# Hybrid-attention trunk: how scores' keys and queries lie in HBM, buffer counts and planner delays

## The chip, the cores and the metric

One NeuronCore of a Trainium2 chip runs the whole program. TensorE (PE) multiplies, with its weight loads shown apart (PEld); VectorE (DVE), ScalarE (ACT) and GpSimd (POOL) do elementwise work; SyncE (SP) issues most DMAs, and GpSimd issues some too. The metric is the device time in microseconds, the median of several runs.

## The reference

One decoder layer on 1024 tokens of width 1024, all in fp32: a norm, one input projection of 2956 columns, three kinds of causal attention with heads of 64, an output projection, a norm and an MLP with a squared ReLU.

```python
h = rms_norm(x, norm_mix);  a_q, a_kv, a_g, b_qkv, c_qkv = split(h @ w_in)
o_a = nsa_mixer(...)             # 4 heads: compressed, selected and windowed keys
o_b = dilated_mixer(...)         # 6 heads in 3 groups, strides 1, 4, 16
o_c = stick_breaking_mixer(...)  # 6 heads: sigmoid weights, running products
x = x + concat(o_a, o_b, o_c) @ w_out
x = x + square(relu(rms_norm(x, norm_mlp) @ w_up)) @ w_down
```

A score of the dilated and stick-breaking heads is q·k over 64 dimensions, for 128 queries by up to 512 keys.

## The kernel before

**Precision.** Each fp32 operand of a matmul is split into a high and a low part of type float32r (`put`, L106): ScalarE makes the high part by a cast (L103), VectorE or GpSimd the low one by a subtraction (L112; L114 with a factor). A product is then three matmuls. For scores (`scores`, L632) the 64 dimensions leave half of the 128 partitions free, so the keys' tile holds the high parts in partitions 0 to 63 and the low parts in 64 to 127. One query tile holds the high part twice, the other the low part twice, and two matmuls (L639, L642) give all four products.

**Stages.** Half 0 means tokens 0 to 511, half 1 the rest. First come input, norm statistics and the first projections (to 50 us). Then the projections of both halves run beside the attention of half 0 (to about 470 us); then the output projection and the MLP of half 0 beside the attention of half 1 (to about 1000 us); then the rest of that MLP, and output projection and MLP of half 1 alone. The projections are matmuls of L250 and L258, the MLP's of L1094 and L1160.

**Through HBM.** Projected q and k of the dilated and stick-breaking heads go to `q_d` and `k_d` in HBM (`spill_qk`, L538: one store of 128 x 512 for the high part, one for the low, rows being two heads of 64), v to `v_d`. The queries of the first mixer's half 1 go to `nq_d`. They come back later as loads issued by GpSimd (`load_heads`, L597; `Nsa.load`): keys by a pattern whose first dimension is high or low (2) and the second the 64 rows, queries by one whose first dimension repeats the same 64 rows (2, step 0), values as 128 plain rows. The loads go to tiles of a pool with 11 slots of 4 KB a partition.

**Raw weights.** `load_w` (L141) fetches a weight group in 2 or 4 parts of 256 KB through 2 raw buffers (`wraw`); a part is asked for by SP, split, and the buffer taken for the part two further on.

**Order.** The Python program plans with a model clock in units of about a microsecond of TensorE. Attention is a list of units: `Sb` (stick-breaking, 256 queries of a head), `Dil` (a dilated head, half of the tokens), `Nsa` (128 queries of two heads). All other matmul work is one generator, the filler, and `spend` gives the filler so many units for each unit of attention, by what is left of both (0.4 to 4). A unit may be loaded when what it needs is in the set `done` (`later` puts it there after a delay) and enough slots are free; its scores come `WAIT` = 8.5 units after the load (`prefetch`, `ready`), and `fill` puts filler there. The framework's scheduler then orders each engine's queue, and every engine and DMA queue works in order.

Of the kernel before, what the change touches and what calls it, by code (L numbers as in the profile page):

```python
# [10 lines left out]
F32 = mybir.dt.float32  # L11
# [4 lines left out]

S, D, HD, DFF = 1024, 1024, 64, 4096
NB = S // 128
EPS = 1e-6
WMAX = 268  # L20
# [39 lines left out]
def tile_trunk(ctx, tc, x, xT, w_in, w_out, w_up, w_down, cw1, cw2, small, t_nsa, t_dil, out):  # L60
# [57 lines left out]
    hctx = ExitStack()  # L118
    slots = actx.enter_context(tc.tile_pool(name="slots", bufs=11))
    ckp = actx.enter_context(tc.tile_pool(name="ck", bufs=10))  # L120
# [20 lines left out]
    def load_w(key):  # L141
# [23 lines left out]
        def load(part):  # L165
            dst = part[1]
            m = dst.shape[1] * (dst.shape[2] if len(dst.shape) == 3 else 1)
            raw = wpool.tile([128, 2 * WMAX], F32, tag="wraw", bufs=2, name="wraw")[:, :m]
            i = nc.sync.dma_start(raw, src[:, part[0]:part[0] + m])
            if clock[0] < 10.0:  # L170
                in_order(i)
            return raw.rearrange("p (k c) -> p k c", c=128) if len(dst.shape) == 3 else raw

        raws = [load(p) for p in parts[:2]]

        def split():
            for i, (_, hi, lo) in enumerate(parts):
                put(hi, lo, raws[i], pool=i % 2 == 1 and len(w_keys) < 14)
                if i + 2 < len(parts):
                    raws.append(load(parts[i + 2]))  # L180
                if i % 2:
                    yield
# [27 lines left out]
    pending = []  # L210
    DMA, SB0 = 4.0, 8.0
    FLIP, START, END = 1.3, 5.0, 2.5
    SLOTS = 11
    live = [2]
# [214 lines left out]
    def nsa_q(W_q, half):  # L429
        v2 = []  # L430
        for i in range(2):
            v2.append((yield from normed_blocks(W_q, 256, 4, 4 * half + 2 * i)))
        if half == 0:
            yield from take(4)

        def fin(p):
            tp = pair_T(v2, 128 * p)
            if half == 1:
                hi, lo = [sg_t("tnq", F32R)[:, :512] for _ in range(2)]
                for i, r in ((0, A), (1, B)):  # L440
                    put(hi[r], lo[r], tp[r], qg[r, 2 * p + i:2 * p + i + 1])
                for part, t in enumerate((hi, lo)):
                    nc.sync.dma_start(nq_d[p, part].rearrange("h d t -> (h d) t"), t.bitcast(F32))
                return
            nsa['q', 0, p] = hi, lo = [slot(n).rearrange("p (h t) -> p h t", h=2) for n in ("nqh", "nql")]
            for i, r in ((0, A), (1, B)):
                put(hi[A, i], lo[A, i], tp[r], qg[r, 2 * p + i:2 * p + i + 1])
                nc.scalar.copy(hi[B, i], hi[A, i].bitcast(F32))
                nc.vector.tensor_copy(lo[B, i], lo[A, i].bitcast(F32))
        for p in range(2):  # L450
            later(6.0, lambda p=p: fin(p))
# [84 lines left out]


    def spill_qk(pair, j, cs, hi, lo):  # L538
        for part, t in enumerate((hi, lo)):
            nc.sync.dma_start((q_d, k_d)[j][pair, part, :, cs], t.bitcast(F32))  # L540

# [50 lines left out]

    def rows_of(t, *dims):

        return bass.AP(tensor=t.tensor, offset=t.offset, ap=[list(d) for d in dims])

    def load_heads(pair, half, heads=(0, 1)):  # L597

        q0, nk = 512 * half, 512 * (half + 1)
        ks = slice(0, nk)  # L600
        n = len(heads)
        hs = slice(heads[0], heads[0] + n)
        halves = lambda t: t.rearrange("p (h s) -> p h s", h=2)
        part, twice = (128 * S, 2), (0, 2)
        if n == 1:
            r = 64 * heads[0]
            qq = halves(slot("qq"))
            for i in range(2):
                nc.gpsimd.dma_start(qq[:, i], rows_of(q_r[pair, i, r:r + 64, q0:q0 + 512], twice, (S, 64), (1, 512)))
# [5 lines left out]
            nc.gpsimd.dma_start(k, rows_of(k_r[pair, 0, r:r + 64, ks], part, (S, 64), (1, nk)))  # L615
            nc.gpsimd.dma_start(v, v_r[pair, heads[0], :, ks])
            return [(qq[:, 0], qq[:, 1], k, v)]
        qh, ql = [halves(slot(nm)) for nm in ("qh", "ql")]
        k, v = [[t[:, 0], t[:, 1]] if half == 0 else [t, slot(nm)]
                for nm in "kv" for t in [halves(slot(nm)) if half == 0 else slot(nm)]]  # L620
        for i, t in enumerate((qh, ql)):
            for h in heads:
                r = 64 * h
                nc.gpsimd.dma_start(t[:, h], rows_of(q_r[pair, i, r:r + 64, q0:q0 + 512], twice, (S, 64), (1, 512)))
        for h in heads:
            r = 64 * h
            nc.gpsimd.dma_start(k[h], rows_of(k_r[pair, 0, r:r + 64, ks], part, (S, 64), (1, nk)))
        for h in heads:
            nc.gpsimd.dma_start(v[h], v_r[pair, h, :, ks])
        return [(qh[:, h], ql[:, h], k[h], v[h]) for h in heads]  # L630

    def scores(qh, ql, n, k, masked=False):  # L632

# [4 lines left out]
        cs = slice(128 * n, 128 * n + 128)  # L638
        nc.tensor.matmul(o, qh[:, cs], k, start=True, stop=False)  # L639
        if masked:  # L640
            nc.tensor.matmul(o[:, w - 128:w], ident_r, ahead, start=False, stop=False)
        nc.tensor.matmul(o, ql[:, cs], k, start=False, stop=True)  # L642
        return ps
# [101 lines left out]
    class Nsa(Unit):  # L745
# [8 lines left out]
        def load(self):  # L754
            if self.slots:
                qs = nsa['q', 1, self.hp] = [slot(nm).rearrange("p (h t) -> p h t", h=2) for nm in ("nqh", "nql")]
                for part, t in enumerate(qs):
                    for i in range(2):
                        nc.gpsimd.dma_start(t[:, i], rows_of(nq_r[self.hp, part, i], (0, 2), (512, 64), (1, 512)))

# [6 lines left out]
        def branch(self, i, chunks, kt, vt, gate, l0):  # L767

            n, h = self.n, 2 * self.hp + i
            (qh, ql), sl, st = [t[:, i] for t in nsa['q', self.half, self.hp]], SLOPES[6 + h], self.st[i]  # L770
            prev = None
            for k, (p, c0, tab) in enumerate(chunks):
                w = p.shape[-1]
                acc = st[:, 4 * l0 + k:4 * l0 + k + 1]
                ps = scores(qh, ql, n % 4, kt[:, c0:c0 + w])
                biased(ps, w, tab, sl, p, acc, prev)
# [55 lines left out]
    class Sb(Unit):  # L832
# [16 lines left out]
        def weights(self, n, c0):  # L849

            qh, ql, k, _ = self.head
# [4 lines left out]
            ps = scores(qh, ql, n % 4, k[:, c0:c0 + w], masked=after is None)  # L856
            nc.scalar.activation(b[:, :w], ps[:, :w], AF.Sigmoid, scale=-0.125)
# [37 lines left out]
    class Dil(Unit):  # L895
# [18 lines left out]
        def probs(self):  # L914
# [9 lines left out]
            for ro in range(4):  # L924
# [9 lines left out]
                for g in (1, 2):  # L934
                    qh, ql, k, _ = hd[g]
                    if half == 0:
# [4 lines left out]
                    acc = acc_t[:, ro:ro + 1] if g == 1 else stP[:, ro, 0:1]  # L941
                    biased(scores(qh, ql, ro, k), w, dtab[:, 256 * g - w:256 * g], 4.0 * sl[g], p, acc, prev)
                    prev = acc
# [8 lines left out]
            nc.sync.dma_start(self.oN, dP.rearrange(nat, p=128))  # L952
            qh, ql, k, _ = hd[0]
            for i in range(4):
# [5 lines left out]
                p = pn[-1][:, 256 * (i % 2):256 * (i % 2) + w]  # L960
                ps = scores(qh, ql, i, k[:, c0:c0 + w])
                biased(ps, w, dtab[:, 256 - w:256], sl[0], p, stN[:, i, 0:1], None)
# [74 lines left out]
    def raw_tile():  # L1037
        if 'mp' in late:
            return late['mp'].tile([128, 512], F32, tag="raw", bufs=4, name="raw")
        return wpool.tile([128, 2 * WMAX], F32, tag="wraw", bufs=2, name="wraw")[:, :512]  # L1040

# [160 lines left out]
    def flag(key):  # L1202
        later(0.0, lambda: done.add(key))

# [7 lines left out]
    def filler():  # L1212
# [7 lines left out]
        in_order(nc.sync.dma_start(dtab, t_dil))  # L1220
        later(SB0, lambda: done.add(('sb', 0)))
        W = next_w()
# [14 lines left out]
        for key, half in per_half:  # L1237
# [52 lines left out]

    LEAD, WAIT, LEAST, MOST = 0.8, 8.5, 0.4, 4.0
    debt = [0.0]
# [168 lines left out]
```

## Time and profile before

| | |
|---|---|
| median of 3 runs | 1473.87 us (1472.23 to 1474.32) |
| profiled execution | 1478.49 us, span 1476.7 us, mean granted clock 0.953 |
| TensorE busy | 1347.3 us (91%) |
| weight loads / VectorE / ScalarE / GpSimd busy | 1156.5 / 836.8 / 647.7 / 684.3 us |
| SP's DMA queue / GpSimd's DMA queue | 136.45 MB / 33.85 MB |

TensorE is the busiest engine, but its share is an average over the stages. "Idle" of an engine in a stretch is the stretch's length less its busy time. [...] "Landing" of a DMA is the time from its issue to the moment when its last byte is told.

### The profile page before, as it was taken

The page shows a single profiled execution, that of the slowest core. Times are in us where ns is not written, and L with a number is a line of the kernel's source. Part 1 is how long each engine was busy: PE and PEld are TensorE (multiplying, and loading weights), DVE is VectorE, ACT ScalarE, POOL GpSimd, SP SyncE. Part 2 cuts the span into 40 slices and gives each one's busy share as a digit, 9 for nine tenths or more (in the row PEclk, how much of TensorE's full clock was granted, in tenths as well). Part 3 has the DMA queues.
Part 4 walks back from the last instruction along what each step waited for, and adds up shares of the span by engine and source line. Part 5 has one row for each costly group of instructions (what it writes and reads, how often), then busy time and mean ns, then how long its engine had stood idle before and what let it go on. Part 6 is the DMA issues. An engine that isn't in the chain of part 4 may idle for free.

```text
span 1476.7 us, 21132 instructions
## 1 busy us (share of the span) xinstructions
PE 1347.3 (91%) x7241; PEld 1156.5 (78%) x7241; DVE 836.8 (57%) x1973; ACT 647.7 (44%) x1453; POOL 684.3 (46%) x614
## 2 busy tenths in 40 slices
PE   8887978688797999999997696999999999999998
PEld 6876978688786887888886585788888888888887
DVE  7365664468566998888885353783453332332333
ACT  6234554357454666555564142553343222222221
POOL 2123224434673424454556252534755555556553
PEclk9999989899798999999999798999999999999999
DMA  5697566852734422244548545224434333333332
GB/s 180 166 187 192 143 148 152 152 134 61 136 95 144 137 62 61 73 119 115 122 113 146 94 110 110 75 62 136 123 111 145 89 100 94 92 100 92 95 100 86
DMA packets 178572, 171.65 MB, mean 116 GB/s; under 512 B 89376, under 2 KB 105248, under 8 KB 178464
## 3 DMA queue, kind: packets, MB, share of 16 engines
q1 hardware_dynamic: 91808, 136.45, 32.5%
q0 software_dynamic: 86656, 33.85, 13.0%
q8 instruction: 57, 0.93, 0.3%
q14 instruction: 51, 0.42, 0.1%
HBM read 142.67 MB, written 27.30 MB: 115 GB/s over the span
## 4 chain that ended last, share of the span: by engine, by line
PE 67%; DMA 13%; DVE 11%; issue 4%; ACT 4%; SPq 1%; POOL 1%; DVEq 0%; ACTq 0%; POOLq 0%
PE pd L1094 25%; PE pd L1160 23%; DMA wraw<-in_w_in_dram 6%; PE pd L250 6%; PE ptp L684 3%; DMA k<-k_d 2%; PE pd L258 2%; PE po L705 2%; PE po L700 2%; PE pscore L642 1%; PE pscore L639 1%; DMA xch<-stx 1%; DMA wraw<-in_cmp_w_dram 1%; ACT whi L103 1%; DVE b L864 1%
## 5 line engine op out<-in xcount | busy, mean ns | idle before, releaser
L112 POOL TENSOR_TENSOR wlo<-raw,whi 128x512 fp32r<-128x512 f32 x264 | 351.1, 1350 | 370.9 <-ACT whi L103 365.6
L1094 PE MATMUL pd<-whi,hid 128*128 128x512 f32 x1120 | 381.6, 401 | 4.1 <-DVE acc L1099 2.6
L1099 DVE SCALAR_TENSOR_TENSOR acc<-pd,rs,acc 128x512 f32<-128x512 f32 x256 | 191.0, 747 | 117.5 <-PE pd L1094 116.6
L1094 PEld LDWEIGHTS pd<-whi,hid 128*128 128x128 f32 x1120 | 212.2, 189 | 51.9 <-DVE acc L1099 4.3
L103 ACT CAST whi<-raw 128x512 fp32r<-128x512 f32 x264 | 150.6, 619 | 180.7 <-issue 87.8
L1094 PE MATMUL pd<-wlo,hid 128*128 128x512 f32 x560 | 221.7, 396 | 0.0
L1160 PE MATMUL pd<-h_hi,whi 128*128 128x512 f32 x512 | 203.2, 397 | 0.2 <-ACT h_hi L105 0.2
L1160 PE MATMUL pd<-h_lo,whi 128*128 128x512 f32 x512 | 203.0, 398 | 0.0
L1160 PE MATMUL pd<-h_hi,wlo 128*128 128x512 f32 x512 | 202.3, 395 | 0.0
L1164 DVE TENSOR_TENSOR sqr<-sqr 128x512 f32<-128x512 f32 x64 | 49.4, 772 | 263.0 <-ACT sqr L1163 262.7
L250 PE MATMUL pd<-whi,hT_hi 128*128 128x256 f32 (+1 forms) x512 | 155.4, 307 | 15.7 <-DVE vs L114 7.4
L250 PE MATMUL pd<-wlo,hT_hi 128*128 128x256 f32 (+1 forms) x512 | 153.1, 300 | 1.4 <-DVE wlo L112 1.4
L250 PE MATMUL pd<-whi,hT_lo 128*128 128x256 f32 (+1 forms) x512 | 151.7, 298 | 0.0
L1163 ACT ACTIVATE sqr<-pd 128x512 f32<-128x512 f32 x64 | 38.2, 597 | 211.6 <-PE pd L1160 211.6
L1094 PEld LDWEIGHTS pd<-wlo,hid 128*128 128x128 f32 x560 | 106.3, 190 | 20.2
L250 PEld LDWEIGHTS pd<-whi,hT_hi 128*128 128x128 f32 x512 | 104.1, 204 | 17.3 <-DVE vs L114 8.0
L1160 PEld LDWEIGHTS pd<-h_hi,wlo 128*128 128x128 f32 x512 | 97.0, 190 | 22.5
L1160 PEld LDWEIGHTS pd<-h_hi,whi 128*128 128x128 f32 x512 | 97.1, 190 | 22.1 <-ACT h_hi L105 0.7
L1160 PEld LDWEIGHTS pd<-h_lo,whi 128*128 128x128 f32 x512 | 96.4, 189 | 21.3
L112 DVE TENSOR_TENSOR pTlo<-ptp,pThi 128x512 fp32r<-128x512 f32 (+2 forms) x160 | 101.1, 638 | 19.5 <-ACT pThi L103 18.5
L250 PEld LDWEIGHTS pd<-wlo,hT_hi 128*128 128x128 f32 x512 | 105.2, 206 | 1.6 <-DVE wlo L112 1.6
L250 PEld LDWEIGHTS pd<-whi,hT_lo 128*128 128x128 f32 x512 | 104.5, 204 | 0.0
(279 smaller groups left out, 2585.7 us busy)
## 6 DMA issues: line engine op xcount, KB each, us to landing
raw<-in_w_down_dram SPq DMA_DIRECT2D x128, 256.0 KB, 2.9
raw<-in_w_up_dram SPq DMA_DIRECT2D x124, 256.0 KB, 2.9
wraw<-in_w_in_dram SPq DMA_DIRECT2D x66, 256.0 KB, 3.0
k<-k_d POOLq DMA_DIRECT2D x12, 512.0 KB, 19.8
v<-v_d POOLq DMA_DIRECT2D x12, 512.0 KB, 16.1
qh<-q_d POOLq DMA_DIRECT2D x20, 256.0 KB, 11.4
ql<-q_d POOLq DMA_DIRECT2D x20, 256.0 KB, 13.0
v_d<-vs SPq DMA_DIRECT2D x32, 128.0 KB, 3.0
```

What stands on the lines that cost most here:

```text
L103: nc.scalar.copy(dst, src)
L112: eng.tensor_tensor(dst_lo, src, dst_hi.bitcast(F32), op=OP.subtract)
L250: nc.tensor.matmul(ps[:, :n], tokens(a, d, tb), b, start=(d == 0 and j == 0), stop=(d == 7 and j == 2))
L258: nc.tensor.matmul(ps, a, b[half][:, d], start=(d == 0 and j == 0), stop=(d == 7 and j == 2))
L684: nc.tensor.transpose(tp[:, off:off + 128], a, ident)
L700: nc.tensor.matmul(po[:, o0:o0 + w], vst, hi[:, src:src + w], start=(e == 0), stop=False)
L705: nc.tensor.matmul(*rest, start=False, stop=last and s not in held)
L1094: nc.tensor.matmul(ps, a[:, cs], b, start=(k == 0), stop=(k == last))
L1099: nc.vector.scalar_tensor_tensor(acc[:, tb, os_], ps, r2[:, t:t + 1], acc[:, tb, os_], op0=OP.mult, op1=OP.add)
L1160: nc.tensor.matmul(ps, a[:, ds], b[:, d], start=(d == 0 and j == 0), stop=(d == 7 and j == 2))
L1163: nc.scalar.activation(h, ps, AF.Relu)
L1164: nc.vector.tensor_tensor(h, h, h, op=OP.mult)
```

## The change

- `q_d`, `k_d` and `nq_d` hold, for each head, 128 rows: 64 of the high part and 64 of the low. Each store of 128 x 512 becomes two of 64 x 512, one for each head (`spill_rows`).
- Loads take plain rows. Keys come as before (high; low). Queries come as `q1` (high; low) and `q2` (low; high), `q2` by two loads of 64 partitions. For half 0 one load serves two heads. Source and destination are both seen as float32.
- Scores are q1·k + q2·k: two matmuls, the same four products.
- 12 slots instead of 11, 4 raw buffers instead of 2, and GpSimd's descriptor space in SBUF is set to 8192 bytes a partition.
- Readiness: `flag(('sb', 1))` and the projections' keys come 8 units late (`SPILL`), 14 for the dilated q and k (6.1 before); the scores of a unit that takes slots come 14 units after its load (`LOAD`) instead of 8.5.

```diff
-    nq_d = dram.tile([2, 2, 2, 64, 512], F32, name="nq_d")
-    q_r, k_r, v_r, nq_r = [t.bitcast(F32R) for t in (q_d, k_d, v_d, nq_d)]
+    nq_d = dram.tile([2, 2, 128, 512], F32, name="nq_d")
...
-            raw = wpool.tile([128, 2 * WMAX], F32, tag="wraw", bufs=2, name="wraw")[:, :m]
+            raw = wpool.tile([128, 2 * WMAX], F32, tag="wraw", bufs=RAWS, name="wraw")[:, :m]
...
-        raws = [load(p) for p in parts[:2]]
+        raws = [load(p) for p in parts[:RAWS]]
...
+    def spill_rows(dst, step, t):
+        for h, rows in ((0, A), (1, B)):
+            ap = bass.AP(tensor=dst.tensor, offset=dst.offset + h * step, ap=[list(e) for e in dst.ap])
+            nc.sync.dma_start(ap, t[rows].bitcast(F32))
+
     def spill_qk(pair, j, cs, hi, lo):
-        for part, t in enumerate((hi, lo)):
-            nc.sync.dma_start((q_d, k_d)[j][pair, part, :, cs], t.bitcast(F32))
+        for rows, t in ((A, hi), (B, lo)):
+            spill_rows((q_d, k_d)[j][pair, 0, rows, cs], 128 * S, t)
...
-    def rows_of(t, *dims):
-        return bass.AP(tensor=t.tensor, offset=t.offset, ap=[list(d) for d in dims])
+    def fetch(t, src):
+        nc.gpsimd.dma_start(t.bitcast(F32), src)
+
+    def fetch_q(q1, q2, src):
+        fetch(q1, src)
+        fetch(q2[A], src[B])
+        fetch(q2[B], src[A])
...
-                nc.gpsimd.dma_start(t[:, h], rows_of(q_r[pair, i, r:r + 64, q0:q0 + 512], twice, (S, 64), (1, 512)))
-            nc.gpsimd.dma_start(k[h], rows_of(k_r[pair, 0, r:r + 64, ks], part, (S, 64), (1, nk)))
-            nc.gpsimd.dma_start(v[h], v_r[pair, h, :, ks])
+        q = [halves(slot(nm)) for nm in ("q1", "q2")]
+        fetch_q(*q, by_head(q_d[pair], qs))
+        for nm, d in (("k", k_d), ("v", v_d)):
+            if half == 0:
+                t = halves(slot(nm))
+                fetch(t, by_head(d[pair], ks))
+                t = [t[:, 0], t[:, 1]]
+            else:
+                t = [slot(nm) for _ in heads]
+                for h in heads:
+                    fetch(t[h], d[pair, h, :, ks])
...
     def flag(key):
-        later(0.0, lambda: done.add(key))
+        later(SPILL, lambda: done.add(key))
...
-            later(6.1 if key[0] == 'dqk' else 0.0, lambda k=(key, half): done.add(k))
+            later(SPILL + 6.0 * (key[0] == 'dqk'), lambda k=(key, half): done.add(k))
...
-            u.ready_at = clock[0] + WAIT
+            u.ready_at = clock[0] + (LOAD if u.slots else WAIT)
...
-    nc = _bacc.Bacc("TRN2", target_bir_lowering=False, num_devices=1)
+    nc = _bacc.Bacc("TRN2", target_bir_lowering=False, num_devices=1, dynamic_dma_scratch_size=8192)
```

## Rows read from the trace of the kernel before

**Rows 1.** Stretches: length, busy us of PE PEld DVE ACT POOL, PEclk, DMA, GB/s.

```profile
50.00:470.00 420.00, 345.01 (x2352) 323.25 (x2353) 247.17 (x763) 200.79 (x523) 169.09 (x183) 0.89 0.62 146
470.00:790.00 320.00, 316.05 (x1744) 269.33 (x1743) 271.47 (x683) 190.37 (x446) 153.03 (x135) 1.00 0.40 105
790.00:910.00 120.00, 84.62 (x401) 70.90 (x400) 50.23 (x133) 34.54 (x79) 45.28 (x44) 0.83 0.63 111
...
1000.00:1476.70 476.70, 472.61 (x2064) 383.45 (x2062) 169.71 (x236) 145.66 (x272) 264.78 (x208) 1.00 0.35 105
```

**Rows 2.** Same view: 14 low-clock stretches from 50 to 470 summed; two later.

```profile
sum 95.50, PE 65.94 PEld 63.08 DVE 54.92 ACT 42.02 POOL 30.49; mean PE 4.71 PEld 4.51 DVE 3.92 ACT 3.00 POOL 2.18
...
808.20:828.70 20.50, 6.03 (x16) 4.74 (x17) 0.00 (x0) 0.00 (x0) 0.97 (x1) 0.50 1.00 126
...
890.20:903.80 13.60, 4.58 (x14) 3.94 (x15) 0.36 (x1) 0.32 (x1) 0.00 (x0) 0.50 0.61 123
```

**Rows 3.** TensorE's waits, whole span: for whom, us in total, times, longest.

```profile
PE pscore L639 <- issue: 19.1, 2, 16.9
PE po L700 <- ACT pThi L103: 19.0, 4, 7.4
PE pscore L639 <- DMA k<-k_d: 18.8, 2, 13.3
```

**Rows 4.** Chain that ended last, by time: start us, us, what.

```profile
99.08 9.88 DMA wraw<-in_cmp_w_dram
...
193.82 12.26 DMA wraw<-in_w_in_dram
...
445.36 10.67 DMA v_d<-vs
...
804.46 16.02 issue
...
879.65 19.44 DMA k<-k_d
...
1034.99 11.15 PE pd L1094 x48
```

**Rows 5.** DMAs of 629, 642, 796, 192, 348, 457 and 66 us: us to landing.

```profile
v<-v_d POOLq DMA_DIRECT2D x1, 512.0 KB, 3.6
...
k<-k_d POOLq DMA_DIRECT2D x1, 512.0 KB, 19.7
...
k<-k_d POOLq DMA_DIRECT2D x2, 512.0 KB, 25.1
...
wraw<-in_w_in_dram SPq DMA_DIRECT2D x2, 256.0 KB, 10.9
...
wraw<-in_w_in_dram SPq DMA_DIRECT2D x2, 256.0 KB, 2.6
...
v_d<-vs SPq DMA_DIRECT2D x4, 128.0 KB, 2.0
...
DMA packets 1467, 1.75 MB, mean 251 GB/s; under 512 B 125, under 2 KB 773, under 8 KB 1467
```

**Rows 6.** Page, DMA issues of the whole span: count, KB, median us to landing.

```profile
v<-v_d POOLq DMA_DIRECT2D x12, 512.0 KB, 16.1
```

**Rows 7.** Page, DMA queue of GpSimd: packets, MB, share of 16 engines.

```profile
q0 software_dynamic: 86656, 33.85, 13.0%
```

**Rows 8.** ScalarE's waits from 60 to 470 us.

```profile
ACT whi L103 <- DMA wraw<-in_w_in_dram: 81.7, 30, 8.9
```

**Rows 9.** GpSimd's groups: count, busy us, mean ns, idle before.

```profile
L627 POOL DMA_DIRECT2D k<-k_d x20 | 16.3, 833 | 24.1 <-DMA k_d<-tlo 13.1 <-PE pscore L642 10.9
...
L629 POOL DMA_DIRECT2D v<-v_d x20 | 12.2, 632 | 25.0 <-DMA v_d<-vs 15.6 <-PE pscore L642 5.9 <-PE po L705 3.5
```

**Rows 10.** The line of the stores: SP's issue, ns min/median/max.

```profile
L540 SPq DMA_DIRECT2D q_d<-thi x12: 320/327/588, 55.5 to 487.2; - x12
```

**Rows 11.** Stretch view from 500 to 620 us.

```profile
500.00:620.00 120.00, 117.22 (x656) 99.60 (x655) 108.78 (x338) 74.89 (x198) 45.59 (x44) 1.00 0.23 67
```

More of the change, by code (lines that the diff above doesn't have):

```diff
@@ L17 @@
 S, D, HD, DFF = 1024, 1024, 64, 4096
+SLOTS = 12
+RAWS = 4
 NB = S // 128
@@ L118, in tile_trunk @@
     hctx = ExitStack()
-    slots = actx.enter_context(tc.tile_pool(name="slots", bufs=11))
+    slots = actx.enter_context(tc.tile_pool(name="slots", bufs=SLOTS))
     ckp = actx.enter_context(tc.tile_pool(name="ck", bufs=10))
@@ L178, in split @@
                 put(hi, lo, raws[i], pool=i % 2 == 1 and len(w_keys) < 14)
-                if i + 2 < len(parts):
-                    raws.append(load(parts[i + 2]))
+                if i + RAWS < len(parts):
+                    raws.append(load(parts[i + RAWS]))
                 if i % 2:
@@ L210, in tile_trunk @@
     pending = []
-    DMA, SB0 = 4.0, 8.0
+    DMA, SPILL = 4.0, 8.0
     FLIP, START, END = 1.3, 5.0, 2.5
-    SLOTS = 11
     live = [2]
@@ L441, in fin @@
                     put(hi[r], lo[r], tp[r], qg[r, 2 * p + i:2 * p + i + 1])
-                for part, t in enumerate((hi, lo)):
-                    nc.sync.dma_start(nq_d[p, part].rearrange("h d t -> (h d) t"), t.bitcast(F32))
+                for rows, t in ((A, hi), (B, lo)):
+                    spill_rows(nq_d[p, 0, rows], 128 * 512, t)
                 return
-            nsa['q', 0, p] = hi, lo = [slot(n).rearrange("p (h t) -> p h t", h=2) for n in ("nqh", "nql")]
+            nsa['q', 0, p] = q1, q2 = [slot(n).rearrange("p (h t) -> p h t", h=2) for n in ("nq1", "nq2")]
             for i, r in ((0, A), (1, B)):
-                put(hi[A, i], lo[A, i], tp[r], qg[r, 2 * p + i:2 * p + i + 1])
-                nc.scalar.copy(hi[B, i], hi[A, i].bitcast(F32))
-                nc.vector.tensor_copy(lo[B, i], lo[A, i].bitcast(F32))
+                put(q1[A, i], q1[B, i], tp[r], qg[r, 2 * p + i:2 * p + i + 1])
+                nc.scalar.copy(q2[B, i], q1[A, i].bitcast(F32))
+                nc.vector.tensor_copy(q2[A, i], q1[B, i].bitcast(F32))
         for p in range(2):
@@ L534, in tile_trunk @@
     t_sel, t_edge, t_cmp, vm = ntab[:, 0:S], ntab[:, S:S + 128], ntab[:, S + 128:S + 192], ntab[:, S + 192:S + 193]
+    def spill_rows(dst, step, t):
+        for h, rows in ((0, A), (1, B)):
+            ap = bass.AP(tensor=dst.tensor, offset=dst.offset + h * step, ap=[list(e) for e in dst.ap])
+            nc.sync.dma_start(ap, t[rows].bitcast(F32))
     def spill_qk(pair, j, cs, hi, lo):
-        for part, t in enumerate((hi, lo)):
-            nc.sync.dma_start((q_d, k_d)[j][pair, part, :, cs], t.bitcast(F32))
+        for rows, t in ((A, hi), (B, lo)):
+            spill_rows((q_d, k_d)[j][pair, 0, rows, cs], 128 * S, t)
     def end_T(src, pair, j, half):
@@ L590, in spill_dqk @@
             later(6.0, lambda j=j, g=g: fin(j, g))
-    def rows_of(t, *dims):
-        return bass.AP(tensor=t.tensor, offset=t.offset, ap=[list(d) for d in dims])
+    def fetch(t, src):
[4 more added lines that the diff above has]
+        fetch(q2[B], src[A])
     def load_heads(pair, half, heads=(0, 1)):
[L599 to L602, printed above, removed]
+        qs, ks = slice(512 * half, 512 * half + 512), slice(0, 512 * half + 512)
         halves = lambda t: t.rearrange("p (h s) -> p h s", h=2)
-        part, twice = (128 * S, 2), (0, 2)
-        if n == 1:
-            r = 64 * heads[0]
+        by_head = lambda d, cs: d[:, :, cs].rearrange("h p s -> p h s")
+        if len(heads) == 1:
+            h = heads[0]
             qq = halves(slot("qq"))
-            for i in range(2):
-                nc.gpsimd.dma_start(qq[:, i], rows_of(q_r[pair, i, r:r + 64, q0:q0 + 512], twice, (S, 64), (1, 512)))
+            fetch_q(qq[:, 0], qq[:, 1], q_d[pair, h, :, qs])
             if half == 0:
@@ L614, in load_heads, with scores @@
                 k, v = slot("k"), slot("v")
-            nc.gpsimd.dma_start(k, rows_of(k_r[pair, 0, r:r + 64, ks], part, (S, 64), (1, nk)))
-            nc.gpsimd.dma_start(v, v_r[pair, heads[0], :, ks])
+            fetch(k, k_d[pair, h, :, ks])
+            fetch(v, v_d[pair, h, :, ks])
             return [(qq[:, 0], qq[:, 1], k, v)]
[L618 to L623, printed above, removed]
-                nc.gpsimd.dma_start(t[:, h], rows_of(q_r[pair, i, r:r + 64, q0:q0 + 512], twice, (S, 64), (1, 512)))
-        for h in heads:
-            r = 64 * h
-            nc.gpsimd.dma_start(k[h], rows_of(k_r[pair, 0, r:r + 64, ks], part, (S, 64), (1, nk)))
-        for h in heads:
-            nc.gpsimd.dma_start(v[h], v_r[pair, h, :, ks])
-        return [(qh[:, h], ql[:, h], k[h], v[h]) for h in heads]
-    def scores(qh, ql, n, k, masked=False):
+        q = [halves(slot(nm)) for nm in ("q1", "q2")]
+        fetch_q(*q, by_head(q_d[pair], qs))
+        kv = []
+        for nm, d in (("k", k_d), ("v", v_d)):
[7 more added lines that the diff above has]
+                    fetch(t[h], d[pair, h, :, ks])
+            kv.append(t)
+        return [(q[0][:, h], q[1][:, h], kv[0][h], kv[1][h]) for h in heads]
+    def scores(q1, q2, n, k, masked=False):
         ps = ps_s()
@@ L755, in load @@
             if self.slots:
[L756 to L759, printed above, removed]
+                qs = nsa['q', 1, self.hp] = [slot(nm).rearrange("p (h t) -> p h t", h=2) for nm in ("nq1", "nq2")]
+                fetch_q(*qs, nq_d[self.hp].rearrange("h p t -> p h t"))
         def end(self):
@@ L769, in branch @@
             n, h = self.n, 2 * self.hp + i
-            (qh, ql), sl, st = [t[:, i] for t in nsa['q', self.half, self.hp]], SLOPES[6 + h], self.st[i]
+            (q1, q2), sl, st = [t[:, i] for t in nsa['q', self.half, self.hp]], SLOPES[6 + h], self.st[i]
             prev = None
@@ L774, in branch @@
                 acc = st[:, 4 * l0 + k:4 * l0 + k + 1]
-                ps = scores(qh, ql, n % 4, kt[:, c0:c0 + w])
+                ps = scores(q1, q2, n % 4, kt[:, c0:c0 + w])
                 biased(ps, w, tab, sl, p, acc, prev)
@@ L849, in weights @@
         def weights(self, n, c0):
-            qh, ql, k, _ = self.head
+            q1, q2, k, _ = self.head
             Wn = 128 * (n + 1)
@@ L855, in weights @@
             after = self.after.get(n)
-            ps = scores(qh, ql, n % 4, k[:, c0:c0 + w], masked=after is None)
+            ps = scores(q1, q2, n % 4, k[:, c0:c0 + w], masked=after is None)
             nc.scalar.activation(b[:, :w], ps[:, :w], AF.Sigmoid, scale=-0.125)
@@ L960, in probs @@
                 p = pn[-1][:, 256 * (i % 2):256 * (i % 2) + w]
-                ps = scores(qh, ql, i, k[:, c0:c0 + w])
+                ps = scores(q1, q2, i, k[:, c0:c0 + w])
                 biased(ps, w, dtab[:, 256 - w:256], sl[0], p, stN[:, i, 0:1], None)
@@ L1039, in raw_tile @@
             return late['mp'].tile([128, 512], F32, tag="raw", bufs=4, name="raw")
-        return wpool.tile([128, 2 * WMAX], F32, tag="wraw", bufs=2, name="wraw")[:, :512]
+        return wpool.tile([128, 2 * WMAX], F32, tag="wraw", bufs=RAWS, name="wraw")[:, :512]
     def load_rows(src, hi, lo):
@@ L1220, in filler @@
         in_order(nc.sync.dma_start(dtab, t_dil))
-        later(SB0, lambda: done.add(('sb', 0)))
+        later(SPILL, lambda: done.add(('sb', 0)))
         W = next_w()
```

12 lines of the change are left out of this document (6 added, 6 removed).

## Prediction

> **What bounds the kernel now.** I read the stretches first. From 1000 us on TensorE is busy 472.61 of 476.70 us at the full granted clock, and from 470 to 790 us 316.05 of 320 [rows 1]: nothing is to be won there. The loss lies in two places. From 50 to 470 us (projections of the mixers, beside the attention of the first 512 tokens) TensorE is busy 345.01 of 420 us at a mean granted clock of 0.89, and from 790 to 910 us 84.62 of 120 at 0.83 [rows 1]. Idle is 75.0 us in the one and 35.4 in the other. [...]
>
> Next, who ends the idle time. TensorE's waits name the score matmul of L639 first: 19.1 us in 2 waits (longest 16.9) put down to "issue", and 18.8 us in 2 waits for the keys' DMA (longest 13.3) [rows 3]. The 16.9 sits at 804 us [rows 4], where two key loads issued at 796 take 25.1 us [rows 5], so it is a wait for keys too. The rest is spread over waits for ScalarE, led by the probabilities' high half (19.0 us, 4 waits) [rows 3]; the chain of waits tells what stood behind those: in 50 to 470 it goes through raw weights and stores that take 9.88, 12.26 and 10.67 us [rows 4]. There are eleven such DMA pieces of 5 us and more in this stretch (beside the keys' first load), 94.0 us together, of which the first, the longest and the last stand there; I leave out the statistics' broadcast and the exchange of softmax statistics, which the change doesn't touch. All eleven lie where GpSimd's loads of q, k and v are in flight.
>
> So I looked at the DMAs. A 512 KB load of values takes 3.6 us when it is alone, at 629 us, and a 512 KB load of keys behind four of q 19.7, at 642 us [rows 5]. The keys' source pattern begins with a dimension of 2 (high, low), as q's does (the same rows twice); the values' pattern begins with the 128 rows. In the median values look nearly as slow (16.1 us) [rows 6], because they mostly queue behind keys and q. The packet count says why: 104 loads of 128 rows each are 13,312 row packets, but the GpSimd queue shows 86,656 [rows 7]. 80 of the 104 loads have the leading 2; shared among them, the surplus (less 16 completion packets a load) is 896 tiny packets each. I read this as data on a few engines and fillers on the rest. Two bad engines delay every other DMA, since a weight load needs them all: a raw weight load takes 2.6 us at 348 us and 10.9 at 192, in the middle of such loads [rows 5]. ScalarE stands first in line for it: its cast waits 81.7 us for raw weights from 60 to 470 us, in 30 waits [rows 8], and what TensorE needs of the attention is queued behind that cast.
>
> **The change part by part.** *Plain-row loads.* Data per load stay; the leading 2 goes. I price keys and q like the values that were alone (3.6 us for 512 KB), and a batch by the 251 GB/s that SP's queue moved from 66 to 73 us [rows 5]. What a first score matmul needs (both q tiles and one head's keys) is 1.5 MB: 6.3 us at that rate and some 2 us of latency, 8 us instead of 19 to 25. At 796.4 + 8 = 804.4 keys are there when TensorE runs dry (804.46 in the chain); at 879.65 + 8 = 887.7 they come 2 us after it runs dry [rows 4]. Of 19.1 + 13.3 = 32.4 us some 30 go, and of the 5.3 us of clock 5: **35 us**. Bounds: 0, if batches of plain rows are as slow as now, and 38.
>
> In 50 to 470 the eleven pieces have 94.0 us; quiet ones of 2.9 us would make 32, so 62 are excess. A batch shrinks from some 16 to 9 us, and a weight load that meets one is delayed by its share of bandwidth (I put it at 5 us), not by the two worst engines: about a quarter of the excess stays, 47 go. Not all is TensorE's: the attention's own sequence of VectorE and ScalarE comes next. I take two thirds, 31 us, and the whole wait for the first keys, 18.8 - 13.3 = 5.5. That is 36.5 of the 75 us idle, and in the same proportion 16 of the 33 us of clock: **52.5 us**. A third instead of two thirds gives (15.7 + 5.5) x 1.44 = 31, all of it 76.
>
> *GpSimd's own time.* The issues fall from 104 to 86 (5 per stick-breaking pair of half 0 instead of 8, 7 in half 1; 10 and 12 per dilated unit instead of 12; 3 instead of 4 for the late queries) and cost 632 ns as for values instead of 833 [rows 9]: 27 us of GpSimd. What queues behind them are the low halves of weights; GpSimd waits for ScalarE there, so I count nothing.
>
> *Stores per head.* 24 stores of q and k and 4 of the late queries become 56. An SP issue of one takes 327 ns at the median [rows 10], so 28 more are 9 us over 430 us, with raw weights behind them on SP's queue. They are issued ahead now by the four buffers, so I count nothing; if they lie in the way, 9 us at most. Four 128 KB stores that SP issued in a row landed in 2.0 us at the median [rows 5]. [...]
>
> *Four raw buffers.* All parts of a weight group are asked for at once, not the later two when the first two are split. That covers a landing that is still late, and is contained in the two thirds. *12 slots* let both stick-breaking pairs of half 1 (6 each) be live together; keys come earlier there, in a stretch where TensorE is full already: nothing. [...]
>
> *Delays.* Readiness is told 8 units later, and scores come 14 instead of 8.5 units after a load that takes slots. Nothing waits on the chip for that; the planner puts that much more projection or MLP ahead, 5.5 units being 5.9 us (0.65 units are three 128x512 matmuls, and 48 of them take 11.15 us [rows 4]). It removes GpSimd's waits for stores that haven't landed. TensorE's work stays the same; the price is that attention comes later and closer together, where VectorE has little room: from 500 to 620 us it is busy 108.78 of 120 us [rows 11]. I charge 4 us (0 to 20).
>
> **The sum.** The profiled execution took 1478.49 us, 4.6 above the median of the runs. 1478.5 - 35 - 52.5 + 4 = 1395; less 4.6, 1390.
>
> **The rivals.** *First: in 50 to 470 something else is late next.* If the attention's sequence through ScalarE and VectorE is hardly shorter than the weight path, only a third or less comes, with 9 us for SP's issues: 1478.5 - 35 - 31 + 9 + 4 - 4.6 = 1421, up to 1452 if nothing comes there. For it: 19.0 us of TensorE's waits name ScalarE's probabilities [rows 3]. Against it: that cast waits behind raw weights [rows 8].
>
> *Second: the stretch empties.* The four buffers and the quicker loads take away all the excess: 1478.5 - 38 - 76 - 4.6 = 1360, and 1339 with the last quarter of the excess.
>
> *Third: the loads don't get faster.* Then only the delays work, 5.9 us in each of the three waits for keys, and some of the GpSimd waits: about 20 us, 1453. For it: the median of values is long too [rows 6]. Against it: the value load that was alone, and the packets [rows 7]. [...]
>
> *Fourth, slower: attention becomes the late party in 50 to 470.* Four batches of half 0 (the second and third stick-breaking pair, two dilated units) can each be put off by 8 + 5.5 units, 54 units or 58 us of projections that run ahead. If none is made up, the projections are through before the attention, the output projection waits for its heads, and TensorE idles for what VectorE needs. Then the 52.5 us don't come, and 58 us plus some 10 us at the low clock are added: 1478.5 - 35 + 68 - 4.6 = 1507. It decides as soon as more than some 35 us net are not made up. Against it: the planner spreads what filler is left over the units left, and about 50 units of projections of half 1 come after the query projection.
>
> **How the numbers follow.** Forecast 1390 (1362 to 1412): 0.50. First rival (1412 to 1452): 0.27. Second (1335 to 1362): 0.10. Third (1445 to 1465): 0.05. Fourth (1480 and more): 0.06. No change within 0.2%, about what a measurement of this kernel can tell: 0.02. The range 1350 to 1445 holds the forecast, nearly all of the first rival and half of the second, 0.81. Faster 0.92, same 0.02, slower 0.06.
>
> **What the next profile shows.** If the load step is right: keys land in 4 to 10 us, the GpSimd queue has about 13,312 + 86 x 16 = 14,700 packets, and L639 waits under 5 us for keys. If the first stretch is right: raw weights rarely take over 6 us, ScalarE's wait for them is under 40 us, and 50 to 470's work is done some 50 us earlier. The delays are wrong if TensorE idles between 450 and 620 us with VectorE full. The whole is wrong if packets fall and landings don't.

## The result and the profile after

The changed kernel takes 1381.47 us (median of 4 runs, 1378.51 to 1386.82) against 1473.05 us before: a ratio of 0.9387, 95% interval 0.9351 to 0.9423. The profiled execution took 1386.82 us, its span is 1385.0 us, 91.7 less than before. In the same span view as [rows 1] (length, busy us of PE, PEld, DVE, ACT and POOL with counts, granted clock as a share of TensorE's full speed, DMA share, GB/s):

```profile
50.00:470.00 420.00, 392.67 (x2726) 365.18 (x2726) 307.61 (x955) 238.97 (x626) 180.52 (x195) 0.95 0.58 162
470.00:790.00 320.00, 312.63 (x1664) 263.86 (x1663) 243.56 (x564) 173.74 (x392) 152.44 (x138) 0.99 0.36 107
790.00:910.00 120.00, 114.10 (x567) 95.13 (x566) 78.88 (x151) 56.66 (x114) 53.84 (x43) 0.96 0.34 91
...
1000.00:1385.00 385.00, 381.15 (x1661) 308.47 (x1659) 135.24 (x188) 116.78 (x219) 208.84 (x164) 1.00 0.33 99
```

TensorE's idle time from 50 to 470 us fell from 75.0 to 27.3 us, from 790 to 910 from 35.4 to 5.9. Between them, 470 to 790, it rose from 3.9 to 7.4. A stretch now holds other work than before (more matmuls in both of the stretches that lose time), so the sum is the safer number: TensorE was idle for 1476.7 - 1347.3 = 129.4 us and is idle for 1385.0 - 1330.7 = 54.3 now, 75 us less.

The low clock (0.50; the traces before and after have 0.50 and 1.00 and nothing between), to be read beside [rows 2], first all its stretches from 50 to 470 us (seven instead of 14), then those from 780 to 900:

```profile
sum 40.80, PE 35.81 PEld 34.70 DVE 26.55 ACT 18.54 POOL 16.77; mean PE 5.12 PEld 4.96 DVE 3.79 ACT 2.65 POOL 2.40
...
sum 13.60, PE 12.53 PEld 10.90 DVE 11.52 ACT 6.40 POOL 3.87; mean PE 4.18 PEld 3.63 DVE 3.84 ACT 2.13 POOL 1.29
```

From 50 to 470 us TensorE works 35.81 us at the clock 0.50 instead of 65.94. Half of such work counts as lost here, which is an estimate: in the trace before, matmuls of 128x256 start 214 ns apart (median) at 0.50 and 118 at 1.00, those of 128x512 427 and 232. So some 15 us are gained there. Over the span, start and end included, it is 52 instead of 87 us, a gain of some 17.5. Idle and clock together make 92.5 us, and the span shrank by 91.7. The number of matmuls that TensorE had behind it at 470 us, 2,584, it has before 410 us now (206 in the first 50 us and 2,389 from 50 to 410).

TensorE's waits, where [rows 3] had 19.1, 19.0 and 18.8 us:

```profile
PE pd L258 <- ACT hT_hi L106: 9.8, 3, 5.7
PE po L708 <- ACT pThi L104: 5.0, 2, 3.5
...
PE pscore L647 <- DMA k<-k_d: 2.1, 1, 2.1
```

The waits for keys are gone but for one of 2.1 us; what leads now is the start of the kernel (L258). The DMAs, as in [rows 5 to 7] (queue: packets, MB, share; then count, KB each, median us to landing). First two lines of the kernel before:

```profile
wraw<-in_w_in_dram SPq DMA_DIRECT2D x66, 256.0 KB, 3.0
k<-k_d POOLq DMA_DIRECT2D x12, 512.0 KB, 19.8
```

Then the changed kernel:

```profile
q0 software_dynamic: 9568, 33.56, 8.1%
...
wraw<-in_w_in_dram SPq DMA_DIRECT2D x66, 256.0 KB, 4.4
k<-k_d POOLq DMA_DIRECT2D x17, 512.0 KB, 5.8
v<-v_d POOLq DMA_DIRECT2D x17, 512.0 KB, 5.7
...
q_d<-thi SPq DMA_DIRECT2D x24, 128.0 KB, 2.4
...
k_d<-tlo SPq DMA_DIRECT2D x24, 128.0 KB, 3.4
```

Keys and values land alike, at 5.8 and 5.7 us (19.8 and 16.1 before), and the queue's packets fell from 86,656 to 9,568. A raw weight load takes longer than before on the median (4.4 us, 3.0 before), since four are asked for at once (3.1 with two, e4). But ScalarE, which waited 81.7 us for them [rows 8], now waits

```profile
ACT whi L104 <- DMA wraw<-in_w_in_dram: 7.2, 3, 5.0
```

7.2 us from 60 to 470 us.

### The profile page after: what moved, and what is told of

It is laid out like the page before. It is cut to its first block, busy times and chain, and to the rows that moved or that the text cites. A ratio compares the mean times of both kernels' runs of the same rounds, so it can differ in the third digit from the quotient of the medians.

```text
span 1385.0 us, 21218 instructions
## 1 busy us (share of the span) xinstructions
PE 1330.7 (96%) x7241; PEld 1139.7 (82%) x7241; DVE 836.0 (60%) x1973; ACT 647.2 (47%) x1453; POOL 656.9 (47%) x596
## 2 busy tenths in 40 slices
DMA packets 102317, 171.37 MB, mean 124 GB/s; under 512 B 18241, under 2 KB 34113, under 8 KB 102209
## 3 DMA queue, kind: packets, MB, share of 16 engines
q0 software_dynamic: 9568, 33.56, 8.1%
## 4 chain that ended last, share of the span: by engine, by line
PE 72%; DVE 14%; DMA 7%; issue 3%; ACT 2%; POOL 1%; SPq 1%; DVEq 0%; POOLq 0%; ACTq 0%
PE pd L1100 26%; PE pd L1166 23%; PE pd L250 8%; PE pd L258 3%; PE ptp L692 3%; PE po L708 2%; PE po L713 2%; DMA xch<-stx 2%; PE pscore L650 2%; PE pscore L647 2%; DVE b L870 1%; DVE pTlo L113 1%; DMA wraw<-in_cmp_w_dram 1%; DVE acc L1108 1%; DMA xr<-in_xT_dram 1%
## 5 line engine op out<-in xcount | busy, mean ns | idle before, releaser
L250 PE MATMUL pd<-whi,hT_hi 128*128 128x256 f32 (+1 forms) x512 | 149.6, 295 | 8.2 <-DVE vs L115 4.4
L250 PE MATMUL pd<-wlo,hT_hi 128*128 128x256 f32 (+1 forms) x512 | 149.1, 292 | 0.4 <-DVE wlo L113 0.4
L104 ACT CAST pThi<-ptp 128x512 fp32r<-128x512 f32 (+2 forms) x160 | 86.9, 553 | 56.1 <-PE ptp L692 50.8
L250 PEld LDWEIGHTS pd<-whi,hT_hi 128*128 128x128 f32 x512 | 100.1, 197 | 9.3 <-DVE vs L115 4.8
L250 PEld LDWEIGHTS pd<-wlo,hT_hi 128*128 128x128 f32 x512 | 101.1, 197 | 0.7 <-DVE wlo L113 0.6
```

Of the source, the lines that this page charges most:

```text
L104: nc.scalar.copy(dst, src)
L250: nc.tensor.matmul(ps[:, :n], tokens(a, d, tb), b, start=(d == 0 and j == 0), stop=(d == 7 and j == 2))
```

## Experiments

Theory one, that of the prediction: a source pattern with a leading dimension of 2 puts a load on few DMA engines, where every other DMA gets stuck; spreading the loads brings most of the gain. Theory two: the buffers and delays bring it by covering late landings, whatever the loads do. Ratios are against the kernel before on the same chip; the runs were taken on several chips, so differences under some 5 us in the times are not told apart. Of the changed kernel's parts, the smaller descriptor space and the view of the loads as float32 were never changed by themselves.

**e1: the leading 2 put back.**

```diff
     def fetch(t, src):
+        ap = [list(e) for e in src.ap]
+        if ap[0][1] == 128 and src.tensor.name != v_d.tensor.name:
+            ap = [[64 * ap[0][0], 2], [ap[0][0], 64]] + ap[1:]
+            src = bass.AP(tensor=src.tensor, offset=src.offset, ap=ap)
         nc.gpsimd.dma_start(t.bitcast(F32), src)
```

> The changed kernel, but the source patterns of the key loads and of the q1 loads begin again with a dimension of 2 (the 64 high rows, then the 64 low ones): same bytes, same rows, same destination, same number of loads; values and q2 stay as they are. Theory one (the leading 2 puts a load on few DMA engines): the GpSimd queue's packets rise from 9,568 by some 900 for each of the 55 or so loads of the two kinds, keys land in 12 to 25 us instead of 5.8, and the time goes back to 1430 to 1470 us. Theory two (delays and buffers brought the gain by covering late landings): 1380 to 1405 us, whatever the landings are.

Measured: 1381.57 us, ratio 0.9370 (0.9335 to 0.9405), and 9,568 packets, to the packet what the changed kernel has. The experiment failed: row 64 follows row 63 at the same step, so the two dimensions fold into one of 128 and the loads are the same. It lies in theory two's range, but it tells nothing between the theories.

**e2: loads, stores and layout alone.** 11 slots, 2 raw buffers, the old descriptor space and delays.

```diff
-SLOTS = 12
-RAWS = 4
+SLOTS = 11
+RAWS = 2
...
-        later(SPILL, lambda: done.add(key))
+        later(0.0, lambda: done.add(key))
...
-    LEAD, WAIT, LOAD, LEAST, MOST = 0.8, 8.5, 14.0, 0.4, 4.0
+    LEAD, WAIT, LOAD, LEAST, MOST = 0.8, 8.5, 8.5, 0.4, 4.0
```

> The changed kernel with the loads and stores alone: 11 slots, 2 raw buffers, the old descriptor space, readiness and scores as early as before. Theory one: most of the gain is here, 1390 to 1415 us, and TensorE's waits for keys stay under 10 us. Theory two: 1440 to 1470 us.

Measured: 1394.42 us, ratio 0.9457 (0.9414 to 0.9501). The loads alone bring 76 us of the 89 by which the run e1, in effect the changed kernel, is ahead of the kernel before. Theory two falls. ScalarE's wait for raw weights from 60 to 470 us:

```profile
ACT whi L104 <- DMA wraw<-in_w_in_dram: 45.9, 21, 6.1
```

It is nearly halved, not gone: with two buffers the later parts of a weight group are still asked for late.

**e3: the old delays in the changed kernel** (readiness and scores as in e2, the rest as changed).

> The changed kernel with the old delays (readiness told at once, scores 8.5 units after a load). Theory one, by its sum: the delays cost TensorE 4 us and take away GpSimd's waits for stores, so 1375 to 1395 us. Theory two: 1400 to 1440 us.

Measured: 1373.04 us, ratio 0.9320 (0.9284 to 0.9356): the fastest kernel of this study, just under the 1375 us that were expected at least, and 0.6% under the changed one, though the two intervals overlap. The delays bring nothing that shows, not even the relief of GpSimd's waits for stores that the prediction told of; those waits before its loads, first in the changed kernel, then in this one (who waited for what, us, times, longest):

```profile
POOL k L600 <- DMA k_d<-tlo: 11.7, 2, 6.3
POOL v L600 <- DMA v_d<-vs: 7.7, 1, 7.7
...
POOL q L600 <- DMA q_d<-tlo: 3.5, 1, 3.5
```

```profile
POOL q L600 <- DMA q_d<-tlo: 11.4, 3, 5.8
POOL v L600 <- DMA v_d<-vs: 8.3, 2, 5.8
POOL k L600 <- DMA k_d<-tlo: 3.7, 1, 3.7
```

22.9 us with the delays, 23.4 without (35.1 before, in 6 waits).

**e4: two raw buffers in the changed kernel.**

```diff
-RAWS = 4
+RAWS = 2
```

> The changed kernel with 2 raw buffers. Theory one: raw weights land nearly on time once the loads are spread, so the buffers are worth 5 to 15 us: 1386 to 1400 us. Theory two: 1410 us and more, with ScalarE's waits for raw weights back over 60 us.

Measured: 1399.76 us, ratio 0.9480 (0.9435 to 0.9525), 18 us over the changed kernel: more than the 5 to 15 expected, and ScalarE's wait comes back nearly to the 60 us of theory two's mark:

```profile
ACT whi L104 <- DMA wraw<-in_w_in_dram: 59.2, 30, 5.0
```

So the wait for raw weights was for the larger part the buffers' to remove: with the spread loads and two buffers it is 59.2 us of the 81.7, although the landings are short here (3.1 us at the median).

**e5 and e6: the leading 2 that can't fold, and its control.** Four empty rows lie between a head's high and low rows in HBM. In e5 a load of q1 or keys has the pattern (2, 64 rows, columns), in e6 it is two loads of 64 plain rows.

```diff
-    q_d, k_d, v_d = [dram.tile([6, 2, 128, S], F32, name=n) for n in ("q_d", "k_d", "v_d")]
+    q_d, k_d, v_d = [dram.tile([6, 2, r, S], F32, name=n) for n, r in (("q_d", 132), ("k_d", 132), ("v_d", 128))]
...
+        head = [[68 * ap[0][0], 2], [ap[0][0], 64]]                    # e5
...
+            nc.gpsimd.dma_start(t[A].bitcast(F32), src[A])             # e6
+            nc.gpsimd.dma_start(t[B].bitcast(F32), src[68:132])
```

> The pattern of the run e1 folded back into 128 plain rows, since row 64 follows row 63. Here four empty rows lie between a head's high and low rows in HBM, so the leading 2 can't fold; the loads of q1 and of keys have it, a load of two heads being two loads. Everything else is the changed kernel. Theory one (a leading 2 puts a load on few engines): the GpSimd queue's packets rise to some 40,000 and more, keys land in 10 to 20 us, and the time is 1420 to 1465 us, the buffers and delays covering a part. Theory two (delays and buffers brought the gain): 1375 to 1400 us.

> The control to the leading 2: the same four empty rows, each load of q1 and of keys as two loads of 64 plain rows. Theory one: some 10,000 packets, landings as in the changed kernel, 1375 to 1395 us. If the distance between the rows or the number of loads mattered: as slow as with the leading 2.

Measured: e5 1433.24 us, ratio 0.9744 (0.9713 to 0.9776); e6 1379.43 us, ratio 0.9391 (0.9367 to 0.9416). The layout, the bytes and the buffers are the same, e5 has fewer loads than e6, and the shape of the pattern alone costs 54 us. e5's queue and landings, then TensorE's waits:

```profile
q0 software_dynamic: 36688, 33.73, 9.7%
...
v<-v_d POOLq DMA_DIRECT2D x17, 512.0 KB, 11.1
k<-k_d POOLq DMA_DIRECT2D x12, 512.0 KB, 18.9
```

```profile
PE pscore L654 <- DMA k<-k_d: 26.5, 4, 10.3
PE pscore L654 <- issue: 9.9, 1, 9.9
```

Keys land in 18.9 us again, values, whose pattern is untouched and which come through the same queue, in 11.1 instead of 5.7; and these two rows are 36.4 us of TensorE's waits for keys. (The one named "issue" is the score matmul that starts at 879.64 us; two key loads issued from 860 to 865 us took 19.0 us.) Time and landings are as theory one has them, the packets fewer than the 40,000 expected (see the last section): 36,688 against

```profile
q0 software_dynamic: 10096, 33.56, 9.4%
...
k<-k_d POOLq DMA_DIRECT2D x34, 256.0 KB, 6.0
```

10,096 in e6, where keys land in 6.0 us. That a load became two of half the partitions costs nothing that can be measured (1379.43 and 1381.47 us).

**e7: everything but the loads.** The kernel before with 12 slots, 4 raw buffers, the small descriptor space and the delays:

```diff
+SLOTS = 12
+RAWS = 4
...
-            raw = wpool.tile([128, 2 * WMAX], F32, tag="wraw", bufs=2, name="wraw")[:, :m]
+            raw = wpool.tile([128, 2 * WMAX], F32, tag="wraw", bufs=RAWS, name="wraw")[:, :m]
...
-            u.ready_at = clock[0] + WAIT
+            u.ready_at = clock[0] + (LOAD if u.slots else WAIT)
```

> The kernel before with all of the change but loads, stores and layout: 12 slots, 4 raw buffers, the small descriptor space, the delays. Theory one: the loads stay slow, buffers and delays cover a part of it, 1425 to 1460 us. Theory two: 1380 to 1410 us.

Measured: 1425.80 us, ratio 0.9697 (0.9660 to 0.9734): 44 us of gain without the loads, at the quick end of what theory one allows. ScalarE's wait for raw weights (60 to 470 us) is gone here too, and TensorE's waits for keys stay:

```profile
ACT whi L105 <- DMA wraw<-in_w_in_dram: 3.3, 3, 2.2
```

```profile
PE pscore L640 <- issue: 14.1, 2, 11.0
PE pscore L640 <- DMA k<-k_d: 12.2, 2, 9.3
```

Loads alone 76 us (e2), the rest alone 44, both 92: some 30 us are won by either.

**e8: the stores as one again.** In the changed kernel, each store of q and k as one of 128 x 512 whose destination begins with the two heads:

```diff
         for rows, t in ((A, hi), (B, lo)):
-            spill_rows((q_d, k_d)[j][pair, 0, rows, cs], 128 * S, t)
+            dst = (q_d, k_d)[j][pair, 0, rows, cs]
+            ap = bass.AP(tensor=dst.tensor, offset=dst.offset, ap=[[128 * S, 2]] + [list(e) for e in dst.ap])
+            nc.sync.dma_start(ap, t.bitcast(F32))
```

> The changed kernel with its q and k stores as one of 128 x 512 again, whose destination begins with a dimension of 2 (the two heads), in place of two of 64 x 512. If SyncE's DMAs suffer from a leading 2 as GpSimd's do: stores of q and k land in 8 to 15 us instead of 2.8, raw weights behind them land late, 1390 to 1440 us, so the stores per head are needed by the layout. If they don't: 1375 to 1390 us, and the split only costs SyncE some issues.

Measured: 1514.77 us, ratio 1.0312 (1.0278 to 1.0347): 133 us over the changed kernel, 45 over the kernel before, and well past what was expected. The chain that ended last (start us, us, what) runs through these stores and the weights behind them:

```profile
63.61 18.67 DMA k_d<-tlo
...
107.25 22.23 DMA wraw<-in_cmp_w_dram x2
...
222.75 18.66 DMA k_d<-tlo
...
253.85 18.56 DMA k_d<-tlo
...
298.43 18.21 DMA k_d<-tlo
...
509.38 18.55 DMA k_d<-tlo
```

Over the whole span, the profile's page gives `k_d<-tlo` 7% of the 1512 us of the chain and `q_d<-thi` 2%. A joined store of 256 KB takes 18 us in it, where the halves land in 2.4 to 3.4 us each at the median (the rows of the changed kernel above). GpSimd waits for them before its loads:

```profile
POOL q L602 <- DMA q_d<-tlo: 65.9, 3, 29.0
POOL k L602 <- DMA k_d<-tlo: 34.4, 3, 17.5
```

SyncE's queue also has fewer packets. First the changed kernel, then this one:

```profile
q1 hardware_dynamic: 92640, 136.45, 34.3%
```

```profile
q1 hardware_dynamic: 91200, 136.45, 28.8%
```

1,440 packets fewer at the same bytes, and by the pages of the two it is packets under 512 bytes that are fewer (16,800 in all queues, 18,241 in the changed kernel). There are 48 DMAs fewer (96 stores of q and k became 48); at 16 packets of 4 bytes that complete each, as the split of the stores added them (52 more DMAs and 832 more packets than the kernel before), they are 768. The other 672 are 14 for each of the 48 joined stores: by this count each is completed by 2 packets instead of 16.

**e9: 11 slots in the changed kernel** (`SLOTS = 11`).

> The changed kernel with 11 slots. The prediction counts the slot at nothing, since keys come earlier where TensorE is full already: 1376 to 1388 us. If the slot is what lets the loads of half 1 start in time: 1395 us and more.

Measured: 1377.90 us, ratio 0.9365 (0.9341 to 0.9389). The slot is worth nothing that shows.

**e10 and e11: which delay.** e10 tells readiness as before and keeps the late scores (`LOAD = 14`); e11 shortens both below the old ones (`LOAD = 5`, the first pair's readiness 5 units after its stores).

> The changed kernel with readiness told at once as before, but scores still 14 units after a load. The kernel with both old delays took 1373 us, the changed one 1381. If the late readiness costs the 8 us: 1370 to 1376 us. If the late scores do: 1378 to 1384 us.

> The changed kernel with still shorter delays: readiness at once, the first pair's 5 units after its stores instead of 8, scores 5 units after a load instead of 8.5 and 14. Loads land in 4 to 8 us, so 5 units (5.4 us) should nearly cover them: 1366 to 1378 us, if attention that comes early is what helps. If loads that aren't there yet stop TensorE again: 1385 us and more, with waits for keys over 10 us.

Measured: e10 1386.72 us, ratio 0.9410 (0.9386 to 0.9434); e11 1379.27 us, ratio 0.9371 (0.9347 to 0.9394). Neither came out as told: e10 lies above both of its ranges, e11 between its two, with 2.3 us of waits for keys, so loads that land late don't stop TensorE there. e10 differs from e3 in one number and their intervals are disjoint: the late scores cost some 13 us when readiness is early, more than both delays together (8 us). The order is not the sum of its parts, and shorter than the old delays is no better: e11 is not told apart from the changed kernel. In the stretch from 50 to 470 us, e3 and then e10:

```profile
50.00:470.00 420.00, 393.60 (x2772) 364.58 (x2772) 327.73 (x980) 242.07 (x636) 184.08 (x199) 0.98 0.59 165
```

```profile
50.00:470.00 420.00, 388.03 (x2710) 360.94 (x2710) 304.89 (x957) 238.02 (x624) 180.35 (x194) 0.95 0.58 162
```

TensorE is idle 5.6 us longer in e10, and its granted clock is 0.95 instead of 0.98. One wait stands out there,

```profile
PE pd L250 <- DVE wlo L113: 9.4, 2, 8.4
```

8.4 us for the low half of a weight. Why the two numbers interact as they do stays open.

**e12: the delays alone, on the kernel before** (readiness 8 units late, 14 for the dilated q and k, scores 14 units after a load).

> The kernel before with the delays alone (readiness 8 units late, 14 for dilated q and k, scores 14 units after a load), loads, slots and buffers as before. The prediction's third rival put them at some 20 us: 1445 to 1462 us. If they gain nothing there either, 1467 to 1480 us; then the 44 us of the run e7 belong to the buffers and the slot.

Measured: 1473.29 us, ratio 1.0019 (0.9998 to 1.0039): no gain. TensorE waits for keys somewhat less (32.0 us; with the wait named "issue" it was 37.9 [rows 3]), but ScalarE waits longer for raw weights from 60 to 470 us, 97.1 us instead of 81.7 [rows 8]:

```profile
PE pscore L639 <- DMA k<-k_d: 32.0, 3, 16.2
```

```profile
ACT whi L103 <- DMA wraw<-in_w_in_dram: 97.1, 35, 13.0
```

So the delays alone are not what gained the 44 us of e7. That leaves the four buffers, alone or with the delays (the slot e9 finds worthless on the spread loads); the buffers were not tried alone on the old loads.

## Why the prediction was right

The forecast was 1390 us; 1381.47 were measured. Its first step held: where the time is lost, and that keys are what the waits named "issue" stood for. **The cause** that the prediction read off the packet surplus is shown by e5 against e6: same bytes, same layout, only the leading 2. Data on a few engines shows in the trace before: from 655 to 661 us, when the key load of 642 us [rows 5] is alone in GpSimd's queue, the queue's packets take 9.0% of 16 engines' time, 1.4 engines, and move 0.20 MB; those of the value load of [rows 5] take all 16 from 632 to 633 us (105.6%, by the packets that start there) and move 0.37 MB in that one us. That it is two engines is an estimate from this and from the packets (last section). That they hold up a weight load fits its completions: a raw weight load ends with 16 packets of 4 bytes, and those of the two asked for at 192.28 and 193.82 us, beside such loads, come from 196.54 to 202.72 us, the 32 together, while those of the load of 348.10 us come from 349.85 to 350.46. That the slow loads hold up the raw weights held in part: the spread loads alone take ScalarE's wait for them from 81.7 to 45.9 us (e2).

**The late stretch** was put at 35 us. The 2 us of latency in it are what short DMAs take in the trace before: 40 stores of 64 KB (`cat_d<-otmp`) land in 2.2 us at the median. From 790 to 1000 us idle went from 38.1 to 5.9 us, and TensorE's work at the low clock there from 20.9 to 9.1 us, half of which is counted: 32 + 6 = 38, and TensorE has no wait over 3 us there.

**The first stretch** was put at 52.5 us, between 31 and 76, and gave 47.7 us of idle and 15 of clock, 63: more than taken, inside the bounds. The 33 and 5.3 us of clock in the two sums take half of TensorE's work at the clock 0.50 (65.94 and 10.61 us [rows 2]) as lost; no run shows that half: by the spacing of the 128x256 matmuls in the trace before (214 and 118 ns) it is 45%, 30 and 4.8 us. The step that fell short is the "two thirds", a guess: waits that ScalarE and VectorE end cost TensorE some 69 us in this stretch before and some 24 now, none of one kind over 5.0 us, so little of the attention's own sequence came next. What brought it is also shared otherwise than told. The prediction let the loads shorten the landings and counted the four buffers as contained in that. But in e4 the landings are short (3.1 us on its page) and ScalarE still waits 59.2 us for raw weights; with four buffers it waits 7.2 us at a median landing of 4.4, and 3.3 us with the old loads (e7). The buffers are worth 18 us on the spread loads. The wait was not only for slow landings, but for parts that were asked for late. One sign that the prediction named failed accordingly: raw weights were rarely to take over 6 us, but in the trace of the changed kernel 27 of the 74 loads of `in_w_in` into a raw buffer do (in the kernel before 14 of the 60 whose landing is told). That the sum still came within 9 us is luck in part: the guessed share stood for the work of the buffers too.

**The delays** were charged 4 us (0 to 20); taking them back gains 8 (e3), as far as overlapping intervals tell that. That they relieve GpSimd of its waits for stores was wrong: 22.9 us with them, 23.4 without. And the third rival's 20 us for them on slow loads are not there: e12 finds none. Of the waits for keys 6 us went there, and ScalarE waited 15 us longer for raw weights; that the one took back the other is likely, but wasn't tried.

**Counted at nothing**: the slot, right (e9). GpSimd's issues: 602 to 665 ns each, as assumed,

```profile
L600 POOL DMA_DIRECT2D q<-q_d x30 | 19.9, 665 | 24.4 <-PE po L713 10.8 <-PE pscore L650 4.2 <-DMA q_d<-tlo 3.5
L600 POOL DMA_DIRECT2D k<-k_d x17 | 10.5, 619 | 20.5 <-DMA k_d<-tlo 11.7 <-PE pscore L650 8.8
L600 POOL DMA_DIRECT2D v<-v_d x17 | 10.2, 602 | 17.0 <-DMA v_d<-vs 7.7 <-DMA wraw<-in_w_in_dram 4.8 <-PE pscore L650 2.8
```

and 86 of them. The added stores were counted wrong: there are 48 stores of q and k before, not 24 (the row of L540 is one of four alike, x12 each), so 52 became 104, and 52 more are 17 us at the prediction's price instead of 9. By the traces SyncE spends 57 us on issuing these stores instead of 22; an issue takes 0.55 us on the mean, and 0.43 before. What that costs no run separates; ScalarE's wait for the raw weights behind them fell all the same.

Joining the halves of the stores again makes a leading 2 in this layout and costs 133 us (e8). For the loads, halves or whole makes no difference (e6).

**The packets** were forecast at 14,700 and are 9,568: rows of 2 KB go two to a packet of 4 KB, so 33.56 MB are 8,192 data packets, and 86 x 16 = 1,376 complete them (the trace has just these two sizes, 4,096 and 4 bytes). In the kernel before, the trace has 10,240 packets of 2,048 bytes. The view as float32 came with the change, and e5, which has it, pairs its rows too. That the view is what pairs them is likely and wasn't tried; the gain doesn't rest on the pairs, for e5 has them and lost 54 us.

**The rivals.** The first (something else next from 50 to 470 us) and the fourth (attention late) did not come: what VectorE and ScalarE still hold up there is some 24 us, and from 450 to 620 us TensorE is busy 166.5 of 170 us. The second (the stretch empties, 1360) came nearer with the old delays, 1373. The third is out, since keys land in 5.8 us instead of 19.8.

## What to carry to other kernels

Read a DMA's price at a load that stands alone, and count packets against rows: the queue with six times the packets that its rows need had loads here of which one, when alone, kept 1.4 of 16 engines busy, and DMAs beside such loads came late (values 11.1 us instead of 5.7 in e5). Make the outermost dimension that can't fold the long one (here 64 or 128 rows), on loads and stores alike, even if one transfer becomes two. And try delays by themselves: these brought nothing that shows, with the slow loads (e12) or with the quick ones (e3).

## What the runs showed of the hardware

A leading dimension of 2 hurts SyncE's stores as it hurts GpSimd's loads: in e8's chain a store of 256 KB took some 18 us, against 2.4 to 3.4 us for a half in the changed kernel, with 14 completion packets fewer for each, and two raw weights in a row behind them took 22.23 us; 8 to 15 us were expected for such a store. Not expected either: two dimensions that are contiguous fold, and the load is then as good as plain (e1: 9,568 packets and 1381.57 us, as the changed kernel has).

The fillers of GpSimd's loads with a leading 2 can be counted. The trace before has 73,344 packets of 4 bytes in GpSimd's queue; less 16 for each of 104 loads that is 896 = 14 x 64 for each of the 80 loads with the leading 2. e5 has 48 such loads and 36,688 - 8,192 - 101 x 16 = 26,880 fillers. It comes out with 896 for each of the 12 loads with rows of 4 KB, and 448 = 14 x 32 for each of the 36 with rows of 2 KB, two to a packet. An estimate from these counts: 2 of the 16 engines carry the 128 or 64 data packets of a load, half each, and each of the other 14 gets one filler for every data packet of such a half. The 1.4 engines of the key load that is alone in the trace before fit that; the records name no engine, so no run shows the two.
